# Closing sums and scaling of an attention tile on other engines, and masked scores one head at a time

## Chip, cores and metric

One core of one Trainium2 chip runs the whole program. The metric is the device time of one execution in microseconds; the time of a kernel is the median of its runs. The engines are TensorE (PE in the rows, its weight loads PEld), VectorE (DVE), ScalarE (ACT), GpSimd (POOL) and SyncE (SP), which here issues the DMAs.

## What is computed

One encoder layer over two sequences of 2048 and 256 rows with 1024 columns, in float32. Half of the mixer's output is differential attention with 4 heads, the other half a bidirectional RWKV7 recurrence with 8 heads of 64; then comes the output projection and a squared-ReLU MLP.

```
h = rms_norm(x);  z = h @ w_in
s = q_blk . k * scale;  p = softmax(s)               # two score maps c = 0, 1 for each head
attn = p[:, :, 0] - lam * p[:, :, 1];  o = attn @ v
o = rms_norm(o, subln_g) * (1.0 - lambda_init)       # over the 128 columns of a head
state = state * w_t + (state . a_t) b_t + v_t k_t;  y = state . r_t    # RWKV7, both directions
x = x + concat(o, y) @ w_out
x + square(relu(rms_norm(x) @ w_ff1)) @ w_ff2
```

## The kernel before

The 18 row tiles of 128 rows (16 and 2) pass through four stages. The projection (`project_stream`) fills DRAM arrays with z, Q, K and V, and `rw_prep` prepares the recurrence beside it. Then `attn_stream` and `rw_units` are merged into one stage: both are generators, and `merge` takes steps of both in a fixed proportion (126 to 277). The last stages are the output projection (`wout`) and the MLP (`mlp`).

In the merged stage the program is recorded in the order of the generators, and a list scheduler of the framework then gives each engine its own order, by its own timeline. An engine works its list strictly in order; a wait holds up all that stands behind it. Any edit to what an engine does can therefore move rows elsewhere in the stage.

Attention takes 72 tiles of 128 query rows (4 heads, 18 row tiles each). `attn_scores` (lines 581 to 596) makes, for each block of 512 keys and each of two maps, a score tile `sc` in PSUM (two matmuls, lines 588 and 589), its negated row maximum `nb` on VectorE (line 591) and `P` = Exp of it on ScalarE (line 595). `attn_combine` (lines 598 to 626) joins the blocks: `l` is the row sum, `cf` and `g` the factors; lines 618 and 620 scale P by cf on ScalarE or GpSimd, and the two maps are joined by line 626 on VectorE or lines 623 and 624 on GpSimd. `attn_pv` transposes P (`atp`, line 632), copies it (`at`, line 634) and multiplies by V into `oo` (line 637), a PSUM tile with one half for each of two successive tiles.

`attn_out` (lines 639 to 650) closes a tile. Line 643 takes the sum of squares `oss` of the output on ScalarE. Lines 645 and 646 make `ors` = l*l*1e-6 + oss/128 on VectorE, line 647 raises it to the power -0.5 on GpSimd, line 649 scales the output by it on VectorE, reading PSUM, and line 650 stores the result `o` (one buffer) to the array MIX.

The recurrence goes by 18 units of a forward and a backward tile. `rw_inter` makes for each the factors `ar` and `bk`, and from these, for each half x of 64 steps, the scores of two halves h of the heads: 4 matmuls of 64 rows each for each h into a PSUM bank `scp` (line 935), masked by VectorE into `sc` (line 938). Before, the two banks were asked for together and the matmuls alternate between h = 0 and h = 1. Then `bk` is transposed into `bp` (line 941) and copied by line 942. The banks of `scp`, `lp`, `bp` and `yp` share one tag with two buffers. `rw_leaf` solves small triangular systems by 31 pairs of steps `ltmp`, `lx` (lines 962, 964) on VectorE and GpSimd, with a round trip through DRAM (`MD`, `XD`) on either side; `rw_merge` and `rw_chain` carry the state on.

Of the kernel before, what the change touches and what calls it, by code (L numbers as in the profile page):

```python
# [8 lines left out]
F32 = mybir.dt.float32  # L9
F32R = mybir.dt.float32r  # L10
ALU = mybir.AluOpType
AF = mybir.ActivationFunctionType
# [45 lines left out]
class K:  # L58
# [580 lines left out]
    def attn_out(self, a):  # L639
        nc, sp, op, l0 = self.nc, self.aw, a["op"], a["l"][:, 0:1]  # L640
        sq = sp.tile([128, 128], F32, name="osq", tag="osq", bufs=1)
        ss = sp.tile([128, 1], F32, name="oss", tag="oss")
        nc.scalar.activation(out=sq, in_=op, func=AF.Square, accum_out=ss)
        rs = sp.tile([128, 1], F32, name="ors", tag="ors")
        nc.vector.scalar_tensor_tensor(out=rs, in0=l0, scalar=1e-6, in1=l0, op0=ALU.mult, op1=ALU.mult)
        nc.vector.scalar_tensor_tensor(out=rs, in0=ss, scalar=1.0 / 128, in1=rs, op0=ALU.mult, op1=ALU.add)
        nc.gpsimd.tensor_tensor(out=rs, in0=rs, in1=self.halfneg[:, 0:1], op=ALU.pow)
        o = sp.tile([128, 128], F32, name="o", tag="ao", bufs=1)
        nc.vector.tensor_scalar(out=o, in0=op, scalar1=rs, scalar2=None, op0=ALU.mult)
        nc.sync.dma_start(out=self.MIX[a["t0"]:a["t0"] + 128, a["h"] * 128:a["h"] * 128 + 128], in_=o)  # L650

    def attn_stream(self):
# [222 lines left out]
    def rw_inter(self, d, t, u, pc):  # L875


        nc, sp, pp = self.nc, self.ru, self.rup
        ts = slice(t * 128, t * 128 + 128)
        eg = self.eg  # L880
        R = self.NR
        tw = sp.tile([65, 128], F32, name="tw", tag="tw")
        nc.sync.dma_start(out=tw, in_=self.TW[:, ts])
        kk = sp.tile([128, 4, 128], F32, name="kk", tag="kk", bufs=1)
        nc.sync.dma_start(out=kk, in_=self.KK[:, :, ts].rearrange("c p t -> p c t"))
        ar = sp.tile([128, 4, 2, 2, 64], F32, name="ar", tag="ar", bufs=R)
        for x in range(2):
            xn = 1 - x if d else x
            nc.sync.dma_start(out=ar[:, :, x, 1], in_=self.RR[:, :, t * 128 + xn * 64:t * 128 + xn * 64 + 64].rearrange("c p t -> p c t"))
        kb = sp.tile([128, 4, 2, 128], F32, name="kb", tag="kb", bufs=1)  # L890
        nc.sync.dma_start(out=kb, in_=self.KB[:, :, :, d, ts])
        lp = pp.tile([128, 4, 128], F32, name="lp", tag="w", bufs=WB)
        for c in range(4):
            nc.tensor.matmul(lp[:, c], self.wup[:, d, c * 128:c * 128 + 128], tw, start=True, stop=True)
        lw = sp.tile([128, 512], F32, name="lw", tag="bk", bufs=1)
        nc.scalar.activation(out=lw, in_=lp.rearrange("p c t -> p (c t)"), func=AF.Tanh, scale=0.5)
        with self.urgent():
            getattr(nc, LWE).tensor_scalar(out=lw, in0=lw, scalar1=CDEC, scalar2=CDEC, op0=ALU.mult, op1=ALU.add)
        en = sp.tile([128, 8, 64], F32, name="en", tag="en", bufs=1)
        nc.vector.tensor_tensor_scan(out=en.rearrange("p a b -> p (a b)"), data0=self.chunk, data1=lw[:, ::-1] if d else lw,  # L900
                                     initial=0.0, op0=ALU.mult, op1=ALU.add)
        g4 = en.rearrange("p (c x) t -> p c x t", c=4)
        nc.scalar.activation(out=eg.rearrange("p (c x) t -> p c x t", c=4)[:, :, :, 1:65], in_=g4[:, ::-1] if d else g4, func=AF.Exp)
        nc.scalar.activation(out=en, in_=en, func=AF.Exp, scale=-1.0)
        if pc is None:
            pc = sp.tile([128, 2, 4, 2], F32, name="pc", tag="pc", bufs=4)
        nc.scalar.copy(pc[:, d].rearrange("p c x -> p (c x)"), eg[:, :, 64])

        def view(x):
            return (x[:, :, ::-1] if d else x).rearrange("p c (x t) -> p c x t", x=2)  # L910

        eg4 = eg.rearrange("p (c x) t -> p c x t", c=4)
        en4 = g4[:, ::-1] if d else g4
        nc.vector.scalar_tensor_tensor(out=ar[:, :, :, 0], in0=view(kk), scalar=-0.5, in1=eg4[:, :, :, 0:64], op0=ALU.mult, op1=ALU.mult)
        er = eg4[:, :, :, 64:0:-1] if d else eg4[:, :, :, 1:65]
        with self.urgent():
            (nc.vector if d else getattr(nc, D0E)).tensor_tensor(out=ar[:, :, :, 1], in0=ar[:, :, :, 1], in1=er, op=ALU.mult)
        bk = sp.tile([128, 4, 2, 2, 64], F32, name="bk", tag="bk", bufs=1)
        for s in range(2):
            if d == 0:  # L920
                with self.urgent():
                    getattr(nc, D0E).tensor_tensor(out=bk[:, :, :, s], in0=view(kb[:, :, s]), in1=en4, op=ALU.mult)
                continue
            k, b = slice(64 - s * 64, 128 - s * 64), slice(s * 64, s * 64 + 64)
            nc.vector.tensor_tensor(out=bk[b, :, :, s], in0=view(kb[b, :, s]), in1=en4[b], op=ALU.mult)
            kx = kb[k, :, s].rearrange("p c (x t) -> p c x t", x=2)
            nc.vector.tensor_tensor(out=bk[k, :, :, s], in0=kx[:, :, ::-1], in1=en4[k, :, :, ::-1], op=ALU.mult)
        sc = sp.tile([128, 2, 8, 128], F32, name="sc", tag="sc", bufs=R)
        bkt = sp.tile([128, 2, 4, 128], F32, name="bkt", tag="bkt", bufs=R)
        for x in range(2):  # L930
            pss = [pp.tile([128, 4, 128], F32, name="scp", tag=SCPT, bufs=WB) for h in range(2)]
            for c in range(4):
                for h in range(2):
                    hs = slice(h * 64, h * 64 + 64)
                    nc.tensor.matmul(pss[h][:, c], bk[hs, c, x].rearrange("p s t -> p (s t)"),
                                     ar[hs, c, x].rearrange("p s t -> p (s t)"), start=True, stop=True)
            for h in range(2):
                nc.vector.tensor_tensor(out=sc[:, h, 4 * x:4 * x + 4], in0=pss[h], in1=self.mask[:, d * (1 + h):d * (1 + h) + 1].to_broadcast([128, 4, 128]), op=ALU.mult)
            bp = pp.tile([128, 4, 128], F32, name="bp", tag="w", bufs=WB)
            for c in range(4):  # L940
                nc.tensor.transpose(bp[:, c], bk[:, c, x].rearrange("p s t -> p (s t)"), self.ident)
            nc.scalar.copy(bkt[:, x], bp)
        md = self.MD[u % 4].rearrange("(d q m) r k -> d q r m k", d=2, q=4)
        for q in range(4):
            nc.sync.dma_start(out=md[d, q], in_=sc[q * 32:q * 32 + 32, q // 2, :, (q % 2) * 32:(q % 2) * 32 + 32])
        return dict(ar=ar, sc=sc, bkt=bkt, pc=pc)
# [259 lines left out]
WB = 2  # L1206
# [21 lines left out]
SCPT = "w"  # L1228
# [86 lines left out]
```

## Time and profile before

| | us |
|---|---|
| median of 3 runs (4057.95 to 4066.89) | 4065.56 |
| profiled execution | 4069.43 |
| its span, first to last instruction | 4067.6 |
| merged stage, about 840 to 2200 | 1360 |

Rows of groups give: line, engine, operation, names, shapes, count, then the busy time in us, the mean of one in ns, and the idle time before them with what ended it. Rows of waits give: who waited, for whom, microseconds in all, times, the longest. The page's slices cut the span into 40 equal parts of 101.7 us; each digit is a tenth of busy time.

### The profile page before, as it was taken

What the parts mean: (1) busy time and instruction counts of PE and PEld (TensorE: products, weight loads), DVE (VectorE), ACT (ScalarE), POOL (GpSimd) and SP (SyncE); (2) the same over time, 40 slices, a digit from 0 to 9 for tenths busy, and PEclk for the clock granted to TensorE, in tenths of its full rate; (3) what the DMA queues carried; (4) which work ended last, traced back from release to release, by engine and by line L of the source; (5) the groups of instructions that cost most, each with busy time, mean ns of one, the idle gap of its engine ahead of it and who ended that gap; (6) DMA issues with size and microseconds to landing.
All of it is one profiled execution on the core that took longest, in us unless ns stands there. A gap on an engine that the chain in (4) does not pass through costs nothing.

```text
span 4067.6 us, 75970 instructions
## 1 busy us (share of the span) xinstructions
PE 3841.0 (94%) x28790; PEld 3428.7 (84%) x28790; DVE 2535.4 (62%) x5080; ACT 1904.9 (47%) x4312; POOL 1249.5 (31%) x1632
## 2 busy tenths in 40 slices
PE   8999998988889888889897999999999999999999
PEld 8999998976777677777776778999999999999998
DVE  4254767679878878788885775444444444444443
ACT  4354555467666656566665224333333333333332
POOL 0023666556656556556554440000000000000000
PEclk9999998999989989889998999999999999999999
DMA  6366666643443343334324376222252222521221
GB/s 188 121 198 194 199 178 195 181 108 73 111 95 83 94 119 90 85 85 112 89 62 151 105 234 200 63 68 67 63 186 63 64 66 65 158 63 63 63 63 39
DMA packets 617558, 458.05 MB, mean 113 GB/s; under 512 B 232498, under 2 KB 569191, under 8 KB 617192
## 3 DMA queue, kind: packets, MB, share of 16 engines
q1 hardware_dynamic: 617192, 453.20, 38.9%
q8 instruction: 227, 3.72, 0.4%
q14 instruction: 139, 1.14, 0.1%
HBM read 323.98 MB, written 129.07 MB: 111 GB/s over the span
## 4 chain that ended last, share of the span: by engine, by line
PE 54%; DVE 11%; POOL 6%; DMA 4%; issue 3%; ACT 2%; SPq 1%; POOLq 0%; DVEq 0%; ACTq 0%
PE ups L102 7%; PE ups L100 7%; PE ups L101 7%; PE yps L102 6%; PE yps L101 6%; PE yps L100 6%; DVE nb L591 2%; PE oo L637 2%; PE wops L101 2%; PE wops L100 2%; PE wops L102 2%; POOL lx L964 1%; DMA XD<-lx 1%; POOL ltmp L962 1%; DVE lx L964 1%
## 5 line engine op out<-in xcount | busy, mean ns | idle before, releaser
L504 DVE TENSOR_TENSOR acc<-yps,acc 128x512 f32<-128x512 f32 x576 | 392.0, 688 | 374.8 <-PE yps L102 374.8
L100 PE MATMUL ups<-h2hi,f_hi 128*128 128x384 f32 x1536 | 515.6, 336 | 0.0
L102 PE MATMUL ups<-h2hi,f_lo 128*128 128x384 f32 x1536 | 515.6, 336 | 0.0
L101 PE MATMUL ups<-h2lo,f_hi 128*128 128x384 f32 x1536 | 515.3, 335 | 0.0
L595 ACT ACTIVATE P<-sc,nb 128x512 f32<-128x512 f32 (+1 forms) x528 | 360.2, 685 | 218.4 <-DVE nb L591 203.2
L101 PE MATMUL yps<-f_lo,uh 128*128 128x512 f32 x1152 | 449.8, 391 | 0.0
L100 PE MATMUL yps<-f_hi,uh 128*128 128x512 f32 x1152 | 449.6, 391 | 0.0
L102 PE MATMUL yps<-f_hi,ul 128*128 128x512 f32 x1152 | 442.8, 391 | 0.0
L137 ACT CAST f_hi<-f_raw 128x1024 fp32r<-128x1024 f32 x96 | 96.2, 1048 | 646.7 <-PE yps L102 645.3
L591 DVE TENSOR_REDUCE nb<-sc 128x1 f32<-128x512 f32 (+1 forms) x528 | 345.2, 671 | 56.7 <-PE sc L589 55.6
L637 PE MATMUL oo<-vv,at 128*128 128x128 f32 x2080 | 307.0, 294 | 31.5 <-ACT at L634 20.6
L637 PEld LDWEIGHTS oo<-vv,at 128*128 128x128 f32 x2080 | 272.1, 202 | 60.9 <-ACT at L634 31.6
L588 PE MATMUL sc<-kt,qq 128*128 128x512 f32 (+1 forms) x528 | 253.3, 480 | 49.0 <-ACT P L595 42.1
L492 DVE TENSOR_TENSOR ul<-u,uh 128x384 fp32r<-128x384 f32 x192 | 106.8, 556 | 299.8 <-ACT uh L491 296.3
L101 PEld LDWEIGHTS ups<-h2lo,f_hi 128*128 128x128 f32 x1536 | 288.2, 188 | 5.7
L102 PEld LDWEIGHTS ups<-h2hi,f_lo 128*128 128x128 f32 x1536 | 288.2, 188 | 5.5
L100 PEld LDWEIGHTS ups<-h2hi,f_hi 128*128 128x128 f32 x1536 | 288.3, 188 | 5.5
L102 PEld LDWEIGHTS yps<-f_hi,ul 128*128 128x128 f32 x1152 | 216.1, 188 | 47.4
L143 DVE SCALAR_TENSOR_TENSOR f_lo<-f_raw,g,f_hi 128x256 fp32r<-128x256 f32 x384 | 168.7, 481 | 138.6 <-ACT f_hi L142 138.5
L100 PE MATMUL mm<-w_hi,hT_hi 128*128 128x256 f32 x864 | 250.2, 290 | 4.9 <-DVE qn L330 4.2
L100 PEld LDWEIGHTS yps<-f_hi,uh 128*128 128x128 f32 x1152 | 216.3, 188 | 39.3
L101 PE MATMUL mm<-w_lo,hT_hi 128*128 128x256 f32 x864 | 249.0, 289 | 0.0
(236 smaller groups left out, 9313.0 us busy)
## 6 DMA issues: line engine op xcount, KB each, us to landing
f_raw<-w_ff SPq DMA_DIRECT2D x192, 256.0 KB
f_raw<-w_ff SPq DMA_DIRECT2D x96, 512.0 KB
w_raw<-w_in SPq DMA_DIRECT2D x104, 256.0 KB
qq<-QT SPq DMA_DIRECT2D x288, 64.0 KB
kb<-KB SPq DMA_DIRECT2D x36, 512.0 KB
ZT<-zs SPq DMA_DIRECT2D x84, 192.0 KB
xt<-x SPq DMA_DIRECT2D x27, 512.0 KB
zr<-ZT SPq DMA_DIRECT2D x18, 516.0 KB
```

The lines of the kernel that those rows point to most:

```text
L100: mm(ps, lh, rh, start=start, stop=False)
L101: mm(ps, lh, rl, start=False, stop=False)
L102: mm(ps, ll, rh, start=False, stop=stop)
L137: nc.scalar.copy(hi[:, ks], raw)
L143: nc.vector.scalar_tensor_tensor(out=lo[:, k], in0=raw[:, k - k0], scalar=gk, in1=hi[:, k].bitcast(F32), op0=ALU.mult, op1=ALU.subtract)
L492: nc.vector.tensor_tensor(out=ul[:, ns], in0=u2, in1=uh[:, ns].bitcast(F32), op=ALU.subtract)
L504: nc.vector.tensor_tensor(out=acc[j][:, cs], in0=ps, in1=acc[j][:, cs], op=ALU.add)
L588: nc.tensor.matmul(sc, qq[:, c, 0], kt, start=True, stop=False)
L591: nc.vector.tensor_reduce(out=m, in_=sc, axis=AX.X, op=ALU.max, negate=True)
L595: nc.scalar.activation(out=P, in_=sc, func=AF.Exp, bias=m, accum_out=(a["ls"][:, hf] if a["nh"] > 1 else a["l"])[:, c:c + 1])
L637: nc.tensor.matmul(a["op"], at[:, b], a["kv"][1][hf][:, b], start=k == 0, stop=k == a["n"] - 1)
L964: e.tensor_tensor(out=X[:, 0:i, k0:16], in0=X[:, 0:i, k0:16], in1=tmp[:, 0:i, 0:n], op=ALU.add)
```

## The change

Lines 645 and 646 become two tensor_scalar instructions on GpSimd, in front of the power that was there already. Line 649, the scaling of the output, becomes an activation on ScalarE. In `rw_inter` one bank is asked for at a time: the four matmuls of one h, their mask, then the other h. The lines behind it have numbers lower by one in the changed kernel.

```
-        nc.vector.scalar_tensor_tensor(out=rs, in0=l0, scalar=1e-6, in1=l0, op0=ALU.mult, op1=ALU.mult)
-        nc.vector.scalar_tensor_tensor(out=rs, in0=ss, scalar=1.0 / 128, in1=rs, op0=ALU.mult, op1=ALU.add)
+        nc.gpsimd.tensor_scalar(out=rs, in0=l0, scalar1=l0, scalar2=1e-6, op0=ALU.mult, op1=ALU.mult)
+        nc.gpsimd.tensor_scalar(out=rs, in0=ss, scalar1=1.0 / 128, scalar2=rs, op0=ALU.mult, op1=ALU.add)
         nc.gpsimd.tensor_tensor(out=rs, in0=rs, in1=self.halfneg[:, 0:1], op=ALU.pow)
         o = sp.tile([128, 128], F32, name="o", tag="ao", bufs=1)
-        nc.vector.tensor_scalar(out=o, in0=op, scalar1=rs, scalar2=None, op0=ALU.mult)
+        nc.scalar.activation(out=o, in_=op, func=AF.Copy, scale=rs)
...
         for x in range(2):
-            pss = [pp.tile([128, 4, 128], F32, name="scp", tag=SCPT, bufs=WB) for h in range(2)]
-            for c in range(4):
-                for h in range(2):
-                    hs = slice(h * 64, h * 64 + 64)
-                    nc.tensor.matmul(pss[h][:, c], bk[hs, c, x].rearrange("p s t -> p (s t)"),
+            for h in range(2):
+                hs = slice(h * 64, h * 64 + 64)
+                ps = pp.tile([128, 4, 128], F32, name="scp", tag=SCPT, bufs=WB)
+                for c in range(4):
+                    nc.tensor.matmul(ps[:, c], bk[hs, c, x].rearrange("p s t -> p (s t)"),
                                      ar[hs, c, x].rearrange("p s t -> p (s t)"), start=True, stop=True)
-            for h in range(2):
-                nc.vector.tensor_tensor(out=sc[:, h, 4 * x:4 * x + 4], in0=pss[h], in1=self.mask[:, d * (1 + h):d * (1 + h) + 1].to_broadcast([128, 4, 128]), op=ALU.mult)
+                nc.vector.tensor_tensor(out=sc[:, h, 4 * x:4 * x + 4], in0=ps, in1=self.mask[:, d * (1 + h):d * (1 + h) + 1].to_broadcast([128, 4, 128]), op=ALU.mult)
```

VectorE in the middle of the stage, before, from the row sum of a tile's P to the joining of its two maps (lines 961 to 964 are steps of the leaf):

```order
L610 RECIPROCAL g<-l 128x1
L645 SCALAR_TENSOR_TENSOR ors<-l 128x1
L962 TENSOR_TENSOR ltmp<-lm,lx 128x20x6
L611 SCALAR_TENSOR_TENSOR g<-g,l,lam 128x1
L591 TENSOR_REDUCE nb<-sc 128x1
L646 SCALAR_TENSOR_TENSOR ors<-oss,ors 128x1
L964 TENSOR_TENSOR lx<-lx,ltmp 128x20x6
L613 TENSOR_SCALAR g<-cf,g 128x4
L591 TENSOR_REDUCE nb<-sc 128x1
L962 TENSOR_TENSOR ltmp<-lm,lx 128x19x7
L626 SCALAR_TENSOR_TENSOR P_16396<-P_16402,g,P_16396 128x512
L626 SCALAR_TENSOR_TENSOR P_16512<-P_16518,g,P_16512 128x512
```

The same tile on VectorE in the changed kernel:

```order
L610 RECIPROCAL g<-l 128x1
L591 TENSOR_REDUCE nb<-sc 128x1 x2
L963 TENSOR_TENSOR lx<-lx,ltmp 128x21x6
L611 SCALAR_TENSOR_TENSOR g<-g,l,lam 128x1
L961 TENSOR_TENSOR ltmp<-lm,lx 128x20x6
L613 TENSOR_SCALAR g<-cf,g 128x4
L963 TENSOR_TENSOR lx<-lx,ltmp 128x20x6
L626 SCALAR_TENSOR_TENSOR P_16396<-P_16402,g,P_16396 128x512
L626 SCALAR_TENSOR_TENSOR P_16512<-P_16518,g,P_16512 128x512
```

The rows of `ors`, one of which waits for ScalarE, no longer stand between the sum and the joining.

GpSimd at the same tile, before:

```order
L620 TENSOR_SCALAR P_16512<-P_16512,cf 128x512
L620 TENSOR_SCALAR P_16535<-P_16535,cf 128x512
L647 TENSOR_TENSOR ors<-ors,halfneg 128x1
L623 TENSOR_SCALAR P_16425<-P_16425,g 128x512
L623 TENSOR_SCALAR P_16541<-P_16541,g 128x512
L624 TENSOR_TENSOR P_16419<-P_16419,P_16425 128x512
L624 TENSOR_TENSOR P_16535<-P_16535,P_16541 128x512
```

and in the changed kernel:

```order
L620 TENSOR_SCALAR P_16512<-P_16512,cf 128x512
L620 TENSOR_SCALAR P_16535<-P_16535,cf 128x512
L922 TENSOR_TENSOR bk<-kb,en 128x8x64 x2
L645 TENSOR_SCALAR ors<-l 128x1
L623 TENSOR_SCALAR P_16425<-P_16425,g 128x512
L623 TENSOR_SCALAR P_16541<-P_16541,g 128x512
L624 TENSOR_TENSOR P_16419<-P_16419,P_16425 128x512
L624 TENSOR_TENSOR P_16535<-P_16535,P_16541 128x512
L646 TENSOR_SCALAR ors<-oss,ors 128x1
L647 TENSOR_TENSOR ors<-ors,halfneg 128x1
```

The power, which needs the sum of squares, has moved from ahead of the joining to behind it here, with the two new steps around it. ScalarE of the changed kernel at this tile:

```order
L643 ACTIVATE osq,oss<-oo 128x128
L634 COPY at<-atp 128x512
L595 ACTIVATE P_16512,ls<-sc,nb 128x512
L649 ACTIVATE o<-oo,ors 128x128
L595 ACTIVATE P_16518,ls<-sc,nb 128x512
L941 COPY bkt<-bp 128x512
```

Here the scaling has come in behind the square, with a copy and an Exp between them and an Exp behind.

TensorE at one tile of the recurrence, before, from the last two of the eight alternating matmuls of x = 0 (`scp_11234` and `scp_11235` are the banks of its two h, `scp_11252` is the first bank of x = 1):

```order
L935 MATMUL scp_11234<-ar_11207,bk_11227 128x128
L935 MATMUL scp_11235<-ar_11207,bk_11227 128x128
L637 MATMUL oo_10005<-vv_10028,at_12837 128x128 x4
L588 MATMUL sc_12964<-kt1_10014,qq_12924 128x512
L589 MATMUL sc_12964<-kt1_10014,qq_12924 128x512
L990 MATMUL mp_10861<-zt_10853,sc_10081 32x32 x16
L588 MATMUL sc_12981<-kt0_10018,qq_12924 128x512
L941 MATMUL bp_11246<-ident_60,bk_11227 128x128 x4
L589 MATMUL sc_12981<-kt0_10018,qq_12924 128x512
L588 MATMUL sc_12987<-kt1_10020,qq_12924 128x512
L589 MATMUL sc_12987<-kt1_10020,qq_12924 128x512
L935 MATMUL scp_11252<-ar_11207,bk_11227 128x128 x4
```

and in the changed kernel:

```order
L935 MATMUL scp_11234<-ar_11207,bk_11227 128x128 x4
L935 MATMUL scp_11240<-ar_11207,bk_11227 128x128 x4
L637 MATMUL oo_10005<-vv_10028,at_12837 128x128 x4
L588 MATMUL sc_12981<-kt0_10018,qq_12924 128x512
L589 MATMUL sc_12981<-kt0_10018,qq_12924 128x512
L588 MATMUL sc_12987<-kt1_10020,qq_12924 128x512
L589 MATMUL sc_12987<-kt1_10020,qq_12924 128x512
L989 MATMUL mp_10861<-zt_10853,sc_10081 32x32 x16
L940 MATMUL bp_11246<-ident_60,bk_11227 128x128 x4
```

The eight alternating matmuls of x = 0 have become two runs of four; those of x = 1 were runs of four before.

## Rows read from the trace of the kernel before

**Rows 1.** The page: 40 slices of the span, and the chain by engine

```profile
PE   8999998988889888889897999999999999999999
DVE  4254767679878878788885775444444444444443
...
PE 54%; DVE 11%; POOL 6%; DMA 4%; issue 3%; ACT 2%; SPq 1%; POOLq 0%; DVEq 0%; ACTq 0%
```

**Rows 2.** Busy time by stretch of the merged stage, its columns ahead

```profile
core 0: us, PE busy (x) PEld busy (x) DVE busy (x) ACT busy (x) POOL busy (x), PEclk, DMA share, GB/s
840.00:2200.00 1360.00, 1195.20 (x13857) 993.55 (x13858) 1107.57 (x2500) 885.74 (x2214) 794.67 (x1167) 0.93 0.38 91
```

**Rows 3.** The chain by line in the stretch 840 to 2200

```profile
by line: issue 8.6%; DVE nb L591 7.0%; PE oo L637 5.7%; POOL lx L964 4.0%; DMA XD<-lx 3.9%; POOL ltmp L962 3.7%; DVE lx L964 3.5%; DVE P L626 3.5%; DVE ltmp L962 3.4%; PE scp L935 3.0%; PE sc L588 3.0%; POOL P L624 3.0%; PE atp L632 2.4%; A
```

**Rows 4.** Groups of instructions in the stretch 840 to 2200

```profile
L645 DVE SCALAR_TENSOR_TENSOR ors<-l 128x1 f32<-128x1 f32 x72 | 17.5, 244 | 0.1
L646 DVE SCALAR_TENSOR_TENSOR ors<-oss,ors 128x1 f32<-128x1 f32 x72 | 19.2, 267 | 18.5 <-ACT osq L643 18.1
L649 DVE TENSOR_SCALAR o<-oo,ors 128x128 f32<-128x128 f32 x72 | 24.6, 342 | 13.5 <-POOL ors L647 11.3 <-DMA MIX<-o 1.9
L647 POOL TENSOR_TENSOR ors<-ors,halfneg 128x1 f32<-128x1 f32 x72 | 42.6, 592 | 119.3 <-DVE ors L646 116.3 <-DVE lx L964 1.7 <-DVE g L610 0.8
L620 POOL TENSOR_SCALAR P<-P,cf 128x512 f32<-128x512 f32 x128 | 98.3, 777 | 163.4 <-ACT cf L606 148.7 <-issue 9.9 <-ACT P L595 1.9
L643 ACT ACTIVATE osq<-oo 128x128 f32<-128x128 f32 x72 | 19.8, 275 | 18.1 <-PE oo L637 17.7
L935 PE MATMUL scp<-ar,bk 64*128 64x128 f32 x1152 | 139.1, 303 | 18.3 <-POOL bk L922 7.8 <-DVE bk L927 4.5 <-ACT bkt L942 3.8
L938 DVE TENSOR_TENSOR sc<-scp,mask 128x512 f32<-128x512 f32 x144 | 96.0, 680 | 15.0 <-PE scp L935 14.7
```

**Rows 5.** Who waited for whom in the stretch 840 to 2200

```profile
ACT P L595 <- DVE nb L591: 199.5, 130, 6.1
...
POOL ors L647 <- DVE ors L646: 116.3, 37, 11.7
...
PEld sc L588 <- ACT P L595: 56.8, 60, 3.9
...
PE sc L588 <- ACT P L595: 40.4, 33, 3.6
...
PEld bp L941 <- DVE sc L938: 22.1, 20, 2.8
...
DVE ors L646 <- ACT osq L643: 18.1, 18, 2.3
...
PEld oo L637 <- DVE o L649: 15.7, 16, 2.0
...
PE bp L941 <- DVE sc L938: 14.4, 13, 2.5
...
DVE o L649 <- POOL ors L647: 11.3, 16, 2.2
...
PE oo L637 <- DVE o L649: 10.4, 12, 1.5
```

**Rows 6.** Two small GpSimd groups of one shape, 840 to 2200

```profile
L964 POOL TENSOR_TENSOR lx<-lx,ltmp 128x16 f32<-128x16 f32 x18 | 6.1, 341 | 1.3
...
L962 POOL TENSOR_TENSOR ltmp<-lm,lx 128x16 f32<-128x16 f32 x18 | 5.0, 278 | 1.2
```

**Rows 7.** Waits of SyncE's DMA queue in the stretch 840 to 2200

```profile
SPq L650 <- DVE o L649: 80.2, 28, 10.4
```

**Rows 8.** TensorE in order of time: start, length, instruction, count

```profile
950.53 1.16 PE L935 MATMUL scp<-ar,bk 64*128 64x128 f32 x16
...
954.56 2.21 PE L935 MATMUL scp<-ar,bk 64*128 64x128 f32 x16
...
1425.72 1.16 PE L935 MATMUL scp<-ar,bk 64*128 64x128 f32 x8
```

## The prediction

> **What bounds the kernel now.** I read the slices of the page first: TensorE is at 9 tenths and more at both ends of the span, and from about 840 to 2200 us, where all four engines share work, it falls to 7 or 8 while VectorE rises to 7 or 8 [rows 1]. Only this stage holds lines that the diff touches. Its table of stretches says that no engine is full there: of 1360 us TensorE is busy for 1195, VectorE for 1108, ScalarE for 886, GpSimd for 795, and the granted clock is 0.93, so part of TensorE's work ran at the lower of its two levels [rows 2].
>
> What ends last is then a question for the chain of waits. Over the whole span it lies 11% on VectorE, 6% on GpSimd and 2% on ScalarE [rows 1], which is 447, 244 and 81 us, nearly all of it in this stage, since TensorE is full elsewhere. I divide by the busy time of the stage to get what a microsecond of work there is worth: VectorE 447/1108 = 0.40, GpSimd 244/795 = 0.31, ScalarE 81/886 = 0.09. For the masked scores' matmuls the chain of the stage has its own row: 3.0% of 1360 = 41 us out of 139 busy, so 0.29 [rows 3, 4]. The waits agree: the Exp of line 595 waits 199.5 us for VectorE's maximum, and TensorE waits 56.8 + 40.4 us for the Exp [rows 5]. A busy VectorE delays the maxima, these the Exps, these TensorE. These weights are shares, not proof that each removed row lies on the chain; they are the weakest part of what follows.
>
> **The change part by part.** *VectorE loses three instructions per tile*, 72 of each: 17.5 + 19.2 + 24.6 = 61.3 us [rows 4]. At 0.40 that is -24.5 us. The bounds are 0 (all of it was cover) and -61.3 (all of it was on the chain).
>
> *VectorE loses two waits.* Line 646 waited 18.1 us for ScalarE's sum of squares and line 649 waited 11.3 us for GpSimd's power [rows 5]. Behind them stood maxima and the combination of line 626, as the order shows for one tile. 29.4 us at 0.40 is -11.8; bounds 0 and -29.4.
>
> *GpSimd gains two small instructions per tile*, 144 in all. Its trace has no TENSOR_SCALAR of 128x1. The nearest by size are the 128x16 steps of the leaf, 278 and 341 ns; the power of 128x1 takes 592 ns, and a TENSOR_SCALAR of 512 elements 777 [rows 4, 6]. I take 0.31 us, the middle of the two 128x16 rows, because the time there falls with size and the power is another operation: 144 x 0.31 = 44.6 us, at 0.31 +13.8. Bounds: 0.28 gives +12, 0.59 gives +26; below zero nothing, since work is only added. The order puts line 645 before the combination of lines 623 and 624 and lines 646 and 647 behind it more often than before, so the long wait of line 647 (116.3 us for VectorE [rows 5]) stays mostly out of the way of the next PV. I give no credit for that. Queued behind lines 646 and 647 are the leaf's steps, the copies into tt and the next scaling by cf.
>
> A sentence on the Trainium skill, GPSIMD Engine Reference, section Engine selection: it puts elementwise work on VectorE and calls GpSimd about 2x slower with two inputs, near line rate with one. The trace goes further for small operands: 592 ns on GpSimd against 244 and 267 on VectorE [rows 4]. With twice VectorE's time, an estimate from that page, each would cost 0.51 us, the two together 74 us, +23 in place of +13.8, and the sum below would be about -1.
>
> *ScalarE gains the scaling*, a 128x128 read of PSUM; the square of the same tile takes 275 ns [rows 4]. 72 x 0.275 = 19.8 us, at 0.09 +1.8. It also takes over the wait for the power, now with Exps queued behind it. The order leaves mostly one or two long ScalarE instructions between the square and the scaling, so I carry over the 11.3 us that VectorE waited, and price it at 0.40 because the Exps are what TensorE waits for: +4.5. Bounds: 0, and 72 x (0.31 + 0.59) = 65 us, +26. TensorE's own wait for the bank of oo (15.7 + 10.4 us for line 649 [rows 5]) changes its releaser from VectorE to ScalarE; the chain behind it has one hop less and one more GpSimd step, so I put it at nothing, between -13 and +13. SyncE issues the store of o in order and waited 80.2 us there for VectorE [rows 7]; the queue still has qq loads and MD stores behind it. With the same o a little earlier or later it is at nothing as well; the cover is that qq is asked for a tile ahead.
>
> *Masked scores, one head after the other.* In the old order 31 of 72 pairs of heads alternate, and the trace shows what this buys: 16 matmul records of two heads take 1.16 us when they alternate and 2.21 us when one head follows the other, at the same clock [rows 8]. All 31 are given up: 31 x 1.05 = 33 us more on TensorE. The first mask is not later, since four matmuls of one head alone also take 1.16 us [rows 8]. The second could start at 1.16 + 0.68 = 1.84, when the first mask ends [rows 4], and now has its scores at 2.21: 0.37 us later, 31 x 0.37 = 11 us that nothing covers. The other 22 us hold up what stands behind on TensorE. There the transposes bp wait 22.1 + 14.4 us for the mask [rows 5], so I let that idle time cover half of the 22. 22 us are left, at 0.29 +6.4. Bounds: 0 with full cover and weightless masks, +33 without cover and at full price. Asking for one bank at a time can also start a head earlier; the trace has no wait that shows this and I count nothing.
>
> The Trainium skill, TensorEngine Tiling (Array Packing), section Key Properties, says that different row tiles load and multiply in parallel, which speaks against this part. By it alone all 72 pairs would be lost, 72 x 1.05 = 76 us, +15 after the same cover and weight; the trace agrees on the pairing but shows 954.56 as a row that did not pair [rows 8].
>
> **The sum.** -24.5 - 11.8 + 13.8 + 1.8 + 4.5 + 6.4 = -9.8 us. The profiled execution took 4069.43 us, 4067.6 of span and 1.8 around it; it would become 4060. The median of the three runs is 3.9 lower, 4065.56, and that gives **4056 us**.
>
> **The rivals.**
> *TensorE takes VectorE's place as what ends last* (slower). Place: the matmuls of line 935, which occupy TensorE 1.05 us longer 31 times. For it: TensorE is busy 88% of the stage, more than any other. Against it: 165 us of idle time in the same stage, and bp's waits right behind. Without the TensorE term the sum is -16.2, so the sign turns when more than 16.2 of the 33 us, about half, end up on the path. With all of it: -16.2 + 33 = +17, 4082 us.
> *ScalarE blocks behind GpSimd* (slower). If GpSimd's long steps, 0.78 us each at line 620 [rows 4], stand ahead of the power, the scaling waits for both closing steps in each tile: 65 us in place of 11.3, +26 in place of +4.5, and the sum becomes +12, 4077 us. For it: GpSimd runs in order and all three steps now follow each other there. Against it: GpSimd is idle for 565 of 1360 us, and one hop over VectorE is gone.
> *The freed time was cover.* The chain goes round through TensorE, GpSimd and the DRAM round trips of the leaf, whose landing XD alone is 3.9% of the stage's chain [rows 3]. Then gains and losses both shrink: 4058 to 4073 us.
>
> The whole stage is put in another order, which also moves the clock; from 0.93 to 0.92 or 0.94 would be about 1195 x 0.01/0.93 = 13 us either way. This widens every case and favours none.
>
> **How the numbers follow.** Forecast 0.40 (4040 to 4058, by itself), cover 0.28, TensorE 0.19, ScalarE 0.13. About 0.2%, 8 us, is what a measurement of this kernel can tell from no change. Faster 0.40, same 0.28, slower 0.19 + 0.13 = 0.32. Low end of the range: VectorE's 90.7 us at 0.7 is -63, with +26 from the other terms -37, 4029. High end: the TensorE rival with GpSimd at 0.59 us a step adds 12 to 4082, less what is unlikely at both ends at once: 4090.
>
> **What would show it.** In the profile of the changed kernel VectorE's busy time of the stage falls by about 61 us and the Exp's wait for the maximum falls below 199.5; GpSimd gains 40 to 85 us; line 935 shows 2.21 us for two heads and no 1.16 with 16 records, and TensorE's busy time rises by about 30 us. The forecast is wrong if the Exp's wait for the maximum stays while waits of ScalarE for the power, or of TensorE's sequence behind line 935, appear in its place; or if the granted clock of the stage leaves 0.93 by more than 0.01.

## The result and the profile after

The changed kernel is slower: 4100.13 us (median, 4095.14 to 4105.74) against 4066.22 us for the kernel before, measured beside it. The ratio is 1.0086, 95% interval 1.0065 to 1.0108, some 35 us. The prediction was 4056 us, its range ended at 4090, and the sign was wrong. A few executions of some kernels took over 100 us longer than the others; ratios leave these out, medians do not.

The page of the changed kernel, the rows that answer to [rows 1]: the slices of two engines and the chain by engine.

```profile
PE   8999999988888889898897999999999999999999
...
DVE  4254767588787878787785776444444444444443
...
PE 57%; DVE 12%; POOL 8%; DMA 5%; issue 3%; ACT 3%; SPq 1%; DVEq 0%; POOLq 0%; ACTq 0%
```

The shares of the chain add up to 89% here and to 81% in [rows 1], because it is followed further back, so TensorE's 57% against 54% shows no shift by itself. Up to 840 us the two profiles run alike (TensorE is busy for 798 us in both); what changed is the merged stage. The same stretch as in [rows 2]:

```profile
core 0: us, PE busy (x) PEld busy (x) DVE busy (x) ACT busy (x) POOL busy (x), PEclk, DMA share, GB/s
840.00:2200.00 1360.00, 1206.30 (x13508) 1000.77 (x13508) 1081.74 (x2277) 891.49 (x2259) 847.10 (x1298) 0.92 0.38 90
```

In 1360 us TensorE got through 13508 matmuls in place of 13857: the stage is slower, not merely longer at its end. Groups of the stage (840 to 2240), beside [rows 4]:

```profile
L935 PE MATMUL scp<-ar,bk 64*128 64x128 f32 x1152 | 157.8, 301 | 18.2 <-DVE bk L927 8.8 <-POOL bk L922 4.8 <-DVE sc L937 4.1
...
L937 DVE TENSOR_TENSOR sc<-scp,mask 128x512 f32<-128x512 f32 x144 | 97.2, 681 | 32.7 <-PE scp L935 32.1
...
L647 POOL TENSOR_TENSOR ors<-ors,halfneg 128x1 f32<-128x1 f32 x72 | 41.5, 576 | 3.7
...
L646 POOL TENSOR_SCALAR ors<-oss,ors 128x1 f32<-128x1 f32 x72 | 30.4, 422 | 111.6 <-ACT osq L643 111.0
...
L645 POOL TENSOR_SCALAR ors<-l 128x1 f32<-128x1 f32 x72 | 28.4, 394 | 30.2 <-DVE l L608 20.2 <-ACT o L649 5.6
...
L649 ACT ACTIVATE o<-oo,ors 128x128 f32<-128x128 f32 x72 | 26.7, 371 | 31.1 <-POOL ors L647 30.7
```

The three groups of 61 us are gone from VectorE. Its busy time over the whole execution fell by 18 us only, from 2535 to 2517, since instructions overlap in part and its leaf steps took 15 us longer. The steps that replace the three groups cost more than it put down: 28.4 + 30.4 = 58.8 us on GpSimd against 44.6, and 26.7 us on ScalarE against 19.8. The matmuls of the scores take 157.8 us against 139.1, 19 more where 33 were expected. Who waited for whom, 840 to 2240, beside [rows 5]:

```profile
ACT P L595 <- DVE nb L591: 162.3, 116, 6.9
...
DVE nb L591 <- PE sc L589: 88.4, 93, 4.3
ACT nat L978 <- DMA xt<-XD: 70.7, 19, 9.2
...
DVE ltmp L961 <- DMA lm<-MD: 37.7, 11, 6.9
...
ACT o L649 <- POOL ors L647: 30.7, 22, 3.6
```

The Exps do wait less for the maxima (199.5 us before). Two waits on DMAs have grown, and the prediction had no term for them: VectorE's first leaf step waits 37.7 us for `lm`, the masked scores that come back from the array MD in DRAM, and ScalarE's `nat` 70.7 us for `xt`, the solved systems coming back from XD. The kernel before, same stretch:

```profile
ACT nat L979 <- DMA xt<-XD: 49.9, 19, 5.8
...
DVE ltmp L962 <- DMA lm<-MD: 7.3, 3, 3.9
```

The profile of before has a span some 10 us longer than that of a copy with the same order (`pin_same`, below), so times of single profiles are read here to 10 us only.

### The profile page after: what moved, and what is told of

Read it like the earlier page. It is cut to its first block, busy times and chain, and to the rows that moved or that the text cites. A ratio compares the mean times of both kernels' runs of the same rounds, so it can differ in the third digit from the quotient of the medians.

```text
span 4095.7 us, 75816 instructions
## 1 busy us (share of the span) xinstructions
PE 3875.5 (95%) x28790; PEld 3455.9 (84%) x28790; DVE 2517.4 (61%) x4864; ACT 1919.3 (47%) x4384; POOL 1309.4 (32%) x1776
## 4 chain that ended last, share of the span: by engine, by line
PE 57%; DVE 12%; POOL 8%; DMA 5%; issue 3%; ACT 3%; SPq 1%; DVEq 0%; POOLq 0%; ACTq 0%
PE ups L100 7%; PE ups L102 7%; PE ups L101 7%; PE yps L102 6%; PE yps L101 6%; PE yps L100 6%; DVE nb L591 2%; PE oo L637 2%; DVE lx L963 2%; DVE ltmp L961 2%; PE scp L935 2%; PE wops L100 2%; PE wops L101 2%; PE wops L102 2%; POOL lx L963 2%
## 5 line engine op out<-in xcount | busy, mean ns | idle before, releaser
L143 DVE SCALAR_TENSOR_TENSOR f_lo<-f_raw,g,f_hi 128x256 fp32r<-128x256 f32 x384 | 168.9, 482 | 139.8 <-ACT f_hi L142 137.4
L101 PEld LDWEIGHTS yps<-f_lo,uh 128*128 128x128 f32 x1152 | 216.2, 188 | 38.6
```

The source lines that it names most:

```text
L101: mm(ps, lh, rl, start=False, stop=False)
L143: nc.vector.scalar_tensor_tensor(out=lo[:, k], in0=raw[:, k - k0], scalar=gk, in1=hi[:, k].bitcast(F32), op0=ALU.mult, op1=ALU.subtract)
```

## Experiments

Ratios are to the kernel before, measured beside it on the same chip; 0.1% is 4 us. Costs in us are taken from the ratios.

**Each part alone, and the order alone.** `attn_only` has the closing sums on GpSimd and the scaling on ScalarE, with the scores as before. `bank_only` has the scores one head after the other, the rest as before. `rwn124` and `rwn128` change nothing but the proportion of the merge, `RWN = 126`, so that the scheduler lays the stage out afresh. The first two are halves of the diff ahead; the others:

```
-RWN = 126
+RWN = 124          # rwn128: 128
```

> Only the closing sums on GpSimd and the scaling on ScalarE; the masked scores alternate as before. Theory 1 (the lost pairing on TensorE makes the loss): 4050 to 4066 us, no slower than before. Theory 2 (GpSimd's steps cost 394 and 422 ns in the changed kernel where 310 were expected, and stand in the way of the leaf and of the scaling): most of the 34 us, 4085 to 4100. Theory 3 (each variant's own order of the merged stage decides): no rule, anything within 40 us of before.

Measured: 4063.27 us, 1.0009 [0.9997, 1.0022].

> Only the masked scores one head after the other; the closing sums and the scaling stay on VectorE. Theory 1: line 935 loses its pairs, TensorE is busy some 20 to 33 us longer, and most of it is on the path: 4085 to 4100 us. Theory 2: at most 10 us over before. Theory 3: as for the other part; the two differences need not add up to 34.

Measured: 4111.96 us, 1.0133 [1.0118, 1.0148].

> Control: the kernel before with the proportion in which the two generators are merged set to 124 in place of 126. No instruction is added, removed or moved to another engine, but the scheduler gives the merged stage another order. Theories 1 and 2: within 8 us of before. Theory 3: it moves by 10 to 40 us, either way.

Measured: 4069.03 us, 1.0026 [1.0014, 1.0038].

> Second control of the same kind, the proportion at 128. Theories 1 and 2: within 8 us of before. Theory 3: it moves by 10 to 40 us, either way, and not as the control at 124 does.

Measured: 4071.58 us, 1.0037 [1.0023, 1.0051].

The bank part alone costs 54 us, more than the whole change and far more than the 33 us of TensorE work it was thought to add; the attention part alone costs nothing that can be told. Theory 1 holds for the attention part only; 4112 us lies beyond its 4100 for the bank part. Laying the stage out afresh moves the time by 11 to 15 us without any change of work. So order had to be separated from work.

**The order held.** The next kernels are built twice: first as before, to read the order in which each engine's instructions were laid out, then with the edit, every engine held to that order. The rule, added behind the recording of the program, orders instructions for the scheduler; `pin_same`, the first of these kernels, has as many instructions on the chip as the kernel before (75970):

```
+    last = {}
+    for n in order:                      # the order of the kernel before, by instruction
+        i = ins.get(n); e = str(i.engine)
+        if e in last:
+            tc.add_manual_dep(i, last[e], mybir.DependencyInfo(mybir.DependencyClass.NoSync, mybir.DependencyReason.DATA), reason="pinned order")
+        last[e] = n
```

`pin_same` has no edit. `pin_unpaired` puts the eight score matmuls of a half head after head into the same eight places. `pin_attn` has the attention part, each moved instruction at the place where VectorE had it; `pin_both` has both.

```
+        for group in scp.values():       # pin_unpaired, pin_both: the eight products of a half
+            where = sorted(at[n] for _, _, n in group)
+            for i, (_, _, n) in zip(where, sorted(group)):   # by head, then by column
+                order[i] = n
```

> The kernel before with every engine's order of instructions held to the order that it already has; nothing else is changed. It is the ground on which the three next runs stand. Theory A (the cost of the bank part is the lost alternation of the two row halves on TensorE), theory B (the order in which the merged stage is laid out decides; each edit shuffles it) and theory C (GpSimd's and ScalarE's longer steps) all expect the time of the kernel before, 4061 us, within 8 us. If it is off by more, the holding itself costs something and the three others are read against this one.

Measured: 4058.41 us, 1.0007 [0.9996, 1.0018]. Holding costs nothing that can be told.

> As the run before it, but in the same places of TensorE's order the eight score products of a half are issued head after head instead of alternating between the two row halves. Both banks are still asked for together, and nothing moves on any other engine. Theory A: 33 us of TensorE work more (31 groups of 16 records, 1.05 us each) and, since the bank part alone cost 51 us, nearly all of it or more on the path: 4090 to 4112. Theory B: only the uncovered share of the chain, under 10 us: 4061 to 4071. Theory C: no change.

Measured: 4060.74 us, 1.0013 [1.0002, 1.0024], 2 us above `pin_same`. The alternation is worth next to nothing here. A score pair of `pin_unpaired` in TensorE's timeline (start, us, count), 16 records of 8 matmuls head after head, and a lone head:

```profile
1223.00 1.71 PE L943 MATMUL scp<-ar,bk 64*128 64x128 f32 x16
1228.78 1.16 PE L943 MATMUL scp<-ar,bk 64*128 64x128 f32 x8
```

Of the 36 groups of 16 records in this trace 29 take 1.71 us, in `pin_same` 26 take 1.16. What a pair loses is 0.55 us, not the 1.05 taken from 954.56 in [rows 8], which was one of the longest. The matmuls of line 935 grow from 137.4 to 152.3 us, and nearly all of it is covered. Theory A, the lost alternation, falls.

> The order of the kernel before is kept, and at the very places where VectorE had them the two closing sums of each attention tile go to GpSimd and the scaling to ScalarE; the score products still alternate. Theory A: no loss, and a gain of up to 25 us from 61 us less on VectorE. Theory B: between -25 and 0 us, since no shuffle spoils the gain: 4036 to 4061. Theory C: slower than the held kernel before by 10 to 20 us, because GpSimd's chain of three steps of 0.4 to 0.6 us ends later: 4071 to 4081.

Measured: 4065.37 us, 1.0021 [1.0012, 1.0031], between the values of theories B and C.

> The order of the kernel before is kept, with both: the closing sums on GpSimd and the scaling on ScalarE, and the score products head after head. It differs from the changed kernel in the order of the merged stage and in the release of the second bank. Theory A: the two effects add, about the changed kernel's 4095. Theory B: well under the changed kernel, 4045 to 4070. Theory C: the sum of pin_attn's loss and little else, 4070 to 4080.

Measured: 4071.99 us, 1.0042 [1.0027, 1.0057]. With the order kept the whole change costs 17 us, about half of the 35; the rest is order, and of the bank part's 54 us nearly all. The held kernels still ask for both banks together; asking for one at a time was not priced by itself, but `bank_pin_sp`, below, does so and costs 12 us in all.

**Is it the draw, and on which engine?** `bank_rwn124` and `bank_rwn128` are `bank_only` with RWN at 124 and 128. `bank_pin_pe` and `bank_pin_sp` are `bank_only` with one engine held to the order of the kernel before, by the rule above, restricted to it:

```
+        if e not in ENG:                 # ("PE",) or ("SP",)
+            continue
```

> The bank part alone, with the merge's number RWN at 124 in place of 126, which draws the order of the merged stage afresh and changes no instruction. With the order of the kernel before kept, the bank part cost 2 us; drawn freely at 126 it cost 51. Theory B1 (head after head leaves the planner a poorer order whatever the draw): again 4100 to 4115. Theory B2 (each draw lands somewhere; 126 with this form was a bad one): 4062 to 4090.

Measured: 4111.47 us, 1.0127 [1.0108, 1.0146].

> As the run before it with RWN at 128. Theory B1: again 4100 to 4115. Theory B2: 4062 to 4090, and not the same as at 124.

Measured: 4106.63 us, 1.0117 [1.0100, 1.0134].

> The bank part alone at 126; TensorE is held to the order of the kernel before (score products head after head in the same places), the other engines are laid out freely around it; ScalarE and the DMA queue then stand nearly as before, VectorE and GpSimd differ in places. Theory P (the 51 us lie in TensorE's order, in which attention products come up to 24 products later): back to 4056 to 4068. Theory V (they lie in the order of VectorE's and GpSimd's steps): 4075 or more.

Measured: 4076.53 us, 1.0040 [1.0027, 1.0052].

> The bank part alone at 126; only the DMA queue of SyncE is held to the order of the kernel before. In the bank part alone VectorE's leaf step waited 50 us for the load of lm, against 7 before. Theory L (the loads were queued too late): back to 4056 to 4070 and that wait under 15 us. Theories P and V: 4080 or more, since TensorE and VectorE still stand as the planner draws them.

Measured: 4073.01 us, 1.0030 [1.0017, 1.0042]; VectorE's wait for `lm` is back at 8.3 us.

Not a bad draw: three draws of the bank part cost 47 to 54 us. And not one engine's own list: holding TensorE's or SyncE's alone brings most of it back, since the other engines are laid out around it. The first falls just on theory V's side, the second between its two values, with the wait as theory L had it; neither settles it. So the common feature of the slow orders was looked for. It is the **lead** of the scores: the time from the end of the last masking of a unit's scores (line 938, `sc`) on VectorE to the unit's first leaf step (`ltmp` of 128x31). Unit 7 (units are counted from 0) in VectorE's timeline, before, and then in `bank_only`:

```profile
1364.94 1.27 DVE L938 TENSOR_TENSOR sc<-scp,mask 128x512 f32<-128x512 f32 x2
...
1402.60 0.21 DVE L962 TENSOR_TENSOR ltmp<-lm,lx 128x31 f32<-128x31 f32 x1 [2.73 <-DMA lx<-eye]
```

```profile
1383.95 0.65 DVE L937 TENSOR_TENSOR sc<-scp,mask 128x512 f32<-128x512 f32 x1
...
1391.62 0.21 DVE L961 TENSOR_TENSOR ltmp<-lm,lx 128x31 f32<-128x31 f32 x1 [4.58 <-DMA lm<-MD]
```

Before, the last mask ends at 1366.2 and the leaf starts 36 us later. In `bank_only` 7.0 us lie between, in which the scores go to DRAM and come back, and for the last 4.58 us VectorE is idle until `lm` has landed; the smallest lead in any trace here is 6.5 us. So without a lead VectorE stands before the leaf until the trip is over. Worked out in the same way for all 18 units of each trace (the held kernels that are left out have medians of 29 to 31 us):

| kernel | ratio | median lead, us | units under 12.5 us | VectorE's wait for lm, us |
|---|---|---|---|---|
| before | 1 | 30.6 | 8 | 7.3 |
| pin_same | 1.0007 | 31.0 | 8 | 7.6 |
| pin_unpaired | 1.0013 | 29.6 | 8 | 7.9 |
| attn_only | 1.0009 | 13.8 | 8 | 29.4 |
| rwn124 | 1.0026 | 26.5 | 8 | 14.0 |
| rwn128 | 1.0037 | 31.1 | 7 | 21.2 |
| bank_pin_sp | 1.0030 | 36.7 | 7 | 8.3 |
| bank_pin_pe | 1.0040 | 26.5 | 8 | 11.3 |
| changed kernel | 1.0086 | 8.9 | 14 | 37.7 |
| bank_rwn128 | 1.0117 | 9.4 | 13 | 34.2 |
| bank_rwn124 | 1.0127 | 8.7 | 13 | 40.8 |
| bank_only | 1.0133 | 7.8 | 13 | 50.0 |

The four slow ones are those in which units 5 to 10 have lost their lead; the last seven units have none in the kernel before either. The wait for `lm` alone is not the price: `attn_only` has 29.4 us of it, 27.7 in the last seven units, and is as fast as before. All this is a correlation only, so the lead was taken away and given back.

**The lead taken away, and given back.** One rule for the scheduler, no instruction changed. `before_nolead` is the kernel before with

```
+    for u in range(3, 11):
+        for i in k.dv["s", u, 1, 1]:             # the last two masks of unit u
+            behind(i, k.dv["z", u - 1, 0])       # stand behind zt of the merge of unit u - 1
```

and `bank_lead` is `bank_only`, `after_lead` the changed kernel, `before_lead` the kernel before, with

```
+    for u in range(2, 18):                       # bank_lead: range(2, 11)
+        behind(k.dv["l", u - 1][-1], k.dv["s", u, 1, 1][-1])   # last VectorE step of leaf u - 1 behind the last mask of unit u
```

> The kernel before with one rule for the planner, no instruction changed and the score products still free to alternate: in units 3 to 10 the last two maskings of a unit's scores stand on VectorE behind the first transpose of the merge of the unit before, which takes from these units the lead of their scores over their leaf step (36 us each in the kernel before). Theory R (the lead hides the way of the scores through memory and back; without it each unit takes some 6 us longer): 4059 plus 8 units of 4 to 7 us, 4090 to 4115. Theory S (the lead only goes with the loss, which lies elsewhere in the order): within 15 us of the kernel before.

Measured: 4095.83 us, 1.0095 [1.0080, 1.0110].

> The bank part alone at 126 (4112 us) with one rule for the planner: in units 2 to 10 the last VectorE step of a unit's leaf stands behind the last masking of the scores of the unit after it, which gives these scores their lead again. Everything else is laid out freely, score products head after head. Theory R: 4059 to 4075, with the wait of VectorE for lm under 20 us in place of 50. Theory S: 4095 or more.

Measured: 4071.69 us, 1.0039 [1.0024, 1.0054], against 1.0133 without the rule.

> The changed kernel with the same rule in all units (2 to 17), also in the last seven, where the kernel before has no lead either. Theory R: 4040 to 4075, the loss of 34 us gone, and more if the last units gain too. Theory S: 4085 or more.

Measured: 4067.28 us, 1.0022 [1.0013, 1.0032], against 1.0086.

> The kernel before with the same rule in units 2 to 17; units 2 to 10 already meet it, so only the last seven change. Theory R in its strong form (a lead shortens any unit): 7 units by 4 to 7 us, 4010 to 4035. In its weak form (there the lead is lost because other work is late, so that forcing it only holds VectorE up): 4055 to 4075. Theory S: anything within 15 us of 4059.

Measured: 4055.76 us, 0.9988 [0.9978, 0.9999].

The waits of `before_nolead`, then of `bank_lead`, then of `after_lead`, 840 to 2240:

```profile
ACT nat L982 <- DMA xt<-XD: 68.2, 20, 5.8
...
DVE ltmp L963 <- DMA lm<-MD: 37.5, 8, 6.9
```

```profile
ACT nat L981 <- DMA xt<-XD: 41.3, 19, 5.2
...
DVE ltmp L962 <- DMA lm<-MD: 11.7, 3, 6.7
```

```profile
ACT nat L981 <- DMA xt<-XD: 41.7, 16, 5.2
```

Taking the lead away makes the kernel before as slow as the changed kernel, with the same two waits (37.5 and 68.2 us; 37.7 and 70.7 there), although its scores alternate (29 of 38 groups of 16 records take 1.16 us) and its attention is untouched. The masks that are put off hold TensorE up little by themselves: `bp` waits 18.6 us for them, against 14.4 in [rows 5]. Giving the lead back takes 38 of the bank part's 54 us and 26 of the changed kernel's 35; no wait of VectorE for `lm` is left in `after_lead`. Median leads are 8.5, 25.2 and 30.7 us. All three came out as theory R expected, in time.

How the loss comes about is not settled, for three reasons. First, a rule lays the rest of the stage out afresh too, worth 11 to 15 us by `rwn124` and `rwn128`.

Second, the arithmetic of the expectation, each unit a little longer, is not how the loss shows. Without the lead the leaves of units 4 to 8 start 5 to 32 us earlier than before, and the attention tiles fall back: the 25th tile's power ends 39 us later in the changed kernel and 49 us later in `bank_only` (1294 us before), and in `before_nolead` the tiles fall back by up to 44 us (the 39th). Behind that the leaves are late too: the last one starts 22 us later than before in the changed kernel and in `before_nolead`, 47 in `bank_only`, and 1 us earlier in `bank_lead` and `after_lead`.

Third, the granted clock falls along with the lead in some of these kernels. Over the whole execution its median is 0.972 in the runs of the kernel before (0.973 beside the held kernels), 0.9645 in those of the changed kernel and 0.9655 in `bank_only`; it is 0.971 again in `bank_lead` and `after_lead`, and 0.9695 in `before_nolead`. Among the runs of the kernel before, 0.001 less goes with 1.8 to 2.8 us more; by that, an estimate, the clock goes with 14 to 21 of the changed kernel's 35 us, but with only 5 to 7 of the 38 in `before_nolead`. In the profiles TensorE is busy 34 us longer in the changed kernel than before (3875.5 and 3841.0 us) and idle no longer; in `before_nolead` it is busy no longer (3837.7 us) and idle 27 us longer. So the order decides the time, but it does not cost the same way in both kernels.

In `before_lead` the last seven units get a lead of 22 to 29 us and the wait for `lm` falls to 0.7 us, but the kernel gains only 5 us. The strong form, that any unit gains from a lead, is wrong. Its trace shows the attention tiles from the 43rd on ending 11 to 28 us earlier than before, and the last leaf starting only 2 us earlier; what holds the leaves there was not tried. Nor was it settled why the scheduler gives the lead up when the heads' scores are written one after the other.

**Which half of the attention part costs?** The order of the kernel before, and only the sums (`pin_sums`) or only the scaling (`pin_scale`) moved.

> The order of the kernel before is kept; only the two closing sums of each attention tile go from VectorE to GpSimd, 36.7 us less on VectorE and 59 us more on GpSimd (72 of 0.39 and 72 of 0.44 us). Theory G (GpSimd takes the gain, since its steps stand on the chain at a weight that grows when they get longer): 4064 to 4072, the whole loss. Theory H (the scaling takes it, since ScalarE gets to it late behind its exponentials and gives the bank of the outputs back late): 4050 to 4058, a gain.

Measured: 4067.63 us, 1.0014 [1.0001, 1.0028].

> The order of the kernel before is kept; only the scaling goes from VectorE to ScalarE, 24.6 us less on VectorE and 26.7 us more on ScalarE. Theory G: 4050 to 4058, since VectorE is the dearer of the two. Theory H: 4064 to 4072, the whole loss, with TensorE's wait for the scaling at some 36 us in place of 27.

Measured: 4053.68 us, 0.9989 [0.9977, 1.0001].

The busy times of the stage, `pin_same` and then `pin_attn`:

```profile
840.00:2240.00 1400.00, 1220.62 (x14016) 1010.89 (x14015) 1141.53 (x2547) 899.19 (x2235) 815.40 (x1181) 0.93 0.40 98
```

```profile
840.00:2240.00 1400.00, 1221.09 (x13991) 1011.61 (x13992) 1090.08 (x2323) 917.88 (x2303) 862.81 (x1323) 0.93 0.39 97
```

And the chain of the stage by line, `pin_same` and then `pin_attn`:

```profile
by line: issue 8.9%; DVE nb L592 7.0%; PE oo L638 4.9%; DMA XD<-lx 4.4%; POOL lx L973 3.8%; DVE lx L973 3.7%; DVE P L627 3.7%; DVE ltmp L971 3.7%; POOL ltmp L971 3.6%; POOL P L625 2.7%; ACT P L596 2.5%; PE sc L589 2.4%; PE scp L943 2.3%; PE
```

```profile
by line: issue 7.1%; PE oo L638 6.3%; DVE nb L592 5.2%; POOL lx L973 4.5%; POOL ltmp L971 4.3%; DMA XD<-lx 4.1%; POOL P L625 3.7%; PE scp L943 3.5%; PE sc L589 3.3%; ACT P L596 3.1%; DVE ltmp L971 3.0%; DVE lx L973 2.8%; POOL P L624 2.6%; P
```

VectorE is relieved of 51 us, and its maxima fall from 7.0 to 5.2% of the chain, its leaf steps from 7.4 to 5.8%. What they leave, others take: GpSimd's leaf steps rise from 7.4 to 8.8%, TensorE's `oo`, `scp` and `sc` from 9.6 to 13.1%. The waits of `pin_attn`, of `pin_sums` and of `pin_scale`, 840 to 2240:

```profile
ACT P L596 <- DVE nb L592: 154.1, 94, 7.6
...
POOL ors L651 <- ACT osq L644: 75.7, 33, 8.4
...
ACT o L657 <- POOL ors L652: 50.4, 34, 4.1
```

```profile
POOL ors L651 <- ACT osq L644: 73.5, 29, 8.7
...
DVE o L655 <- POOL ors L652: 27.4, 27, 3.4
```

```profile
ACT o L657 <- POOL ors L652: 39.9, 28, 3.8
```

Both came out as theory G expected. Of the two halves the sums are the dearer, 1.0014 against 0.9989, some 10 us, though they take 37 us off VectorE; next to the 1.0007 of `pin_same` their cost by itself is within the noise. Whoever scales the output waits longer for GpSimd behind them (27.4 us in `pin_sums`, 10.6 in `pin_same`; 50.4 in `pin_attn`, 39.9 in `pin_scale`). The scaling alone on ScalarE is 4 us under the kernel before, with an interval that just holds 1.

Best were `before_lead` and `pin_scale`, each some 5 us under the kernel before; no version's measured time was lower by more than 0.2%.

## Why the prediction was wrong, by its own steps

**The step that failed is the one on the new layout of the stage.** The prediction knew that the stage "is put in another order", priced that at one point of clock, about 13 us either way, and gave it no side. It was the largest term: of the bank part's 54 us all but 5, of the whole change's 35 about half by `pin_both`, 26 by `after_lead`. What the runs show in its place is that the new order masks the scores of units 5 to 10 some 8 to 11 us ahead of their leaf, where the old one left 27 to 38: without that lead the kernel before is slower by 38 us, and with it back the changed kernel keeps 9 of its 35. The clock of the stage moved by one point, 0.92 against 0.93, as the prediction allowed, but over the whole execution it goes with 14 to 21 us by the estimate above, and not with 13 at most. The vanished lead could have been read ahead: on VectorE the rows between a unit's last mask and its first leaf step number 61, 49, 58, 55, 58, 57, 28 for units 4 to 10 before, and 7, 9, 3, 3, 5, 6, 4 after (counted in the traces). The third rival named the place ("the DRAM round trips of the leaf") but only as a brake on gains and losses; it was never asked whether the change uncovers a trip. Three signs that the prediction named came true while the time went the other way, since none of them looks at the layout: the Exp's wait fell to 162.3 us, GpSimd gained 52 us in the stage, and TensorE was busy 34 us longer.

**The lost alternation** was counted with the right number of pairs and a wrong price: 0.55 us, not 1.05, because a row was taken for typical that was among the longest. Its 17 us are nearly all covered, 2 us against +6.4. The rival that gave TensorE the end, 4082 us, came nearest to the measured time, but by pairs that cost 2 us when only they are given up; that is luck. The Trainium skill, TensorEngine Tiling (Array Packing), section Key Properties, says that different tiles can load and multiply in parallel; the +15 that the prediction worked out from it for all 72 pairs was rightly not taken.

**VectorE's removal** was right as work: instructions of 61 us went, 51 us of busy time with the order kept. At 0.40 it was to be worth 24.5 us, with the waits 36. The share of the chain per busy microsecond did not hold for this change; with the order kept, the chain went over to GpSimd, TensorE and ScalarE at once, and the whole attention part, to which the sum gave -16, cost 8 us (1.0021). The slices of TensorE in the stage read 8 and 9, not 7 or 8 as the prediction has it; no term rests on that.

**GpSimd's small steps** took 394 and 422 ns, between the 0.31 us taken and the upper bound of 0.59; 58.8 us in place of 44.6. The kernel before had a row nearer in kind, `tt`, a TENSOR_SCALAR of 32x256 at 448 ns. At 0.31 the difference is +4 to the sum; but they also stand in series before the scaling, and `pin_sums` shows no gain from the 37 us that they free. The Trainium skill, GPSIMD Engine Reference, section Engine selection, calls GpSimd about twice as slow for two inputs; the estimate from that was 0.51 us, and the rows lie between it and 0.31.

**ScalarE's scaling** takes 371 ns, not the 275 of the square of the same tile, 26.7 us; its wait for the power is 30.7 us (50.4 with the order kept) against 11.3 carried over, inside the bounds. By itself it costs nothing (`pin_scale`), so the rival of ScalarE blocked behind GpSimd, at 65 us of waiting, is not what happened.

**The range** was built from the terms that were counted; the layout, which reached some 49 us in the bank part, was put at 13 and had no part in its ends, so the upper one, 4090, was short by 10.

## What to carry to other kernels

Where a scheduler lays out the order, compare the orders first: for each transfer on a loop of dependences (scores to DRAM and back), count what stands between its start and its first reader in either kernel, and look for a vanished cover before pricing any edited instruction. To price an edit, hold the order and change the work, then hold the work and change the order; in the bank part here order cost some 49 us and work 5, in the whole change about half each. Work taken off the engine with the largest share of the chain was worth less than that share here (`pin_attn`), where what replaces it runs in series on the next engines.

## What was not expected of the hardware

An instruction of GpSimd on 128x1 with a scalar for each row takes 394 or 422 ns in the changed kernel, longer than its steps on 128x16 (278 and 341 ns, [rows 6]). Two heads of four matmuls on the two row halves take 1.16 us alternating, 1.71 us one after the other, and 1.16 us for one head alone, so the second head of a sequential pair adds 0.55 us. Scaling a 128x128 tile from PSUM on ScalarE takes 371 ns, squaring it 275.
